# Issuing two weight scalings of a two-layer trunk behind the fourth token tile's rows

## The chip, the cores and the metric

The kernel runs on one core of a Trainium2 chip. The metric is the device time of one execution in microseconds (us); the value given is the median of the runs. A core has a matrix engine (TensorE, "PE" in the profile, its weight loads "PEld"), a vector engine (VectorE, "DVE"), an activation engine (ScalarE, "ACT"), a general engine (GpSimd, "POOL") and an engine that issues the loads and stores here (SyncE, "SP"). Each engine works through its own list of instructions; between engines they wait on semaphores.

## The reference

The input x has 512 tokens of 1024 features. Two layers follow, each a token mixer and a SwiGLU feed-forward net; in front of each sits an RMS normalization and behind each another, with a residual sum. Layer 0 mixes with RWKV-7, layer 1 with a spatial gating unit. The change lies in the first steps of layer 0:

```python
h = _rmsnorm(x, norm_gains[0, 0])
xx = _token_shift(h) - h
xs = h[None] + xx[None] * mix[:, None, None, :]      # six mixtures
r, k, v = jnp.einsum('cbtd,cde->cbte', xs[:3], w_rkv)
xw, xa, xg = xs[3], xs[4], xs[5]
w_raw = w0 + jnp.tanh(xw @ w1) @ w2                  # low rank, 64 wide
a = sigmoid(a0 + (xa @ a1) @ a2)                     # low rank, 64 wide
g = sigmoid(xg @ g1) @ g2
...                                                  # scan over the tokens, group norm, output gate
```

## The kernel before

The 512 tokens are handled as four tiles of 128 (TT = 4), the 1024 features as eight blocks of 128 (KT = 8). Nearly all matrix products are made of three: each factor is split into a rounded part (`whi`, `xgs`, cast on ScalarE, L183) and a rest (`wlo`, subtracted on VectorE, L184).

The function `rwkv` opens layer 0. L742 and L743 load the two low-rank weights w1 and a1 side by side into one tile `w1` (the profile calls it w). The loop at L748 goes over the four token tiles: sums of squares on ScalarE (L253), the inverse root in five small steps on both engines (`rc`, `rh`, `rr`, `rm`, `rt`, `ry`, L260 to L274), and then the scaled rows `hn`. Their left half is made by VectorE in two pieces of 256 columns (L753), the right half by ScalarE (L754). TensorE transposes the rows in eight blocks (`ptr`, L283); VectorE copies the first four out to `h` with the gains (L762), ScalarE the other four (L760). `h` holds all tokens with the features on the partitions, so what reads a block of `h` over all tokens needs all four tiles.

Behind the loop the feature vectors are turned (`vecT`), and `omix` = 1 − mix is formed (L775). At L802 to L805 the low-rank weights are scaled by the mixing factors, once by `omix` and once by `mix`, into two tiles `w1m` of 128 x 1024 on VectorE: the token shift is taken into the weights, so that h times the first plus shifted h times the second is the mixture times the weight. TensorE adds up the 32 products in `lora` (L809), the first 16 with the first tile, the last 16 with the second; ScalarE's tanh and a split give `hid`, which `early` multiplies with the second low-rank weights (`wa`, loaded at L900 and L901 through one buffer, split as `wa2h` and `wa2l`).

`g_hidden` (L837) then loads and splits the gate weight (`wraw` from `rwkv_g`, and its last 32 columns `g1b`, split as `g1s`) and makes its mixture block by block: `xs` on ScalarE and VectorE (L782, L783), split as `xgs`, multiplied into `gA` and `gB`. After it come the mixtures for k and r (`xsp`), with the weights of `rwkv_w_rkv` (`wraw`), and `proj`.

The order of each engine's instructions isn't the order of the text. A planner lays out the whole program once, while it is built, from its own estimates of when operands and loads will be there; on the chip each engine then keeps to its list, whether or not a load has landed. Two calls bind it. `tc.keep_in_program_order(x)` puts x behind the instruction that the text has last before it on the same engine. `with tc.issue_after(y)` puts what the block issues on y's engine behind y. Both bind the order of issue only and add no wait for the end of an instruction. Before the change each of the two scalings is bound by the first call: the first behind `omix`, the second behind the first.

Of the kernel before, what the change touches and what calls it, by code (L numbers as in the profile page):

```python
# [10 lines left out]
AF = mybir.ActivationFunctionType  # L11
ALU = mybir.AluOpType

P = 128
T = 512
D = 1024
KT = D // P
# [116 lines left out]
class Trunk:  # L134
# [551 lines left out]
    def rwkv(self, x0):  # L686
        nc, i, tc = self.nc, self.i, self.tc
        v, a, g = nc.vector, nc.scalar, nc.gpsimd
        mm = nc.tensor.matmul
        with ExitStack() as ctx:  # L690
# [14 lines left out]
            def e2(name, shape=(P, 2, T), dt=F32):  # L705
                return rp.tile(list(shape), dt, name=name, tag="e2", bufs=E2)

            def s4(name, shape, dt=F32):
                return self.slot(shape, dt, name)
# [31 lines left out]
            w1 = s4("w1", [P, KT, 2, 64])  # L741
# [6 lines left out]
            for tt in range(TT):  # L748
                hn = e2("hn", (P, D))
                s = [self.sumsq(x0[tt][:, c:c + 512], hn[:, c:c + 512]) for c in (0, 512)]  # L750
                y = self.rsqrt1(s[1], self.part(s[0], 1.0 / D, RMS_EPS), 1.0 / D)
                for c in (0, 256):
                    v.tensor_scalar(hn[:, c:c + 256], x0[tt][:, c:c + 256], y[:, 0:1], None, op0=ALU.mult)  # L753
                a.activation(hn[:, 512:1024], x0[tt][:, 512:1024], AF.Copy, scale=y[:, 0:1])  # L754
                for q, srcs in enumerate(self.rows_T(hn, lambda n: self.bank("pe", n))):
                    for kt, src in srcs:
                        dst = h[kt // 2][:, kt % 2, 1 + tt * P:1 + (tt + 1) * P]
                        gn = self.vec["g00"][:, kt:kt + 1]
                        if q:
                            a.activation(dst, src, AF.Copy, scale=gn)  # L760
                        else:
                            v.tensor_scalar(dst, src, gn, None, op0=ALU.mult)  # L762
# [39 lines left out]
            w1m = [s4("w1m", [P, KT, 2, 64]) for _ in range(2)]  # L802
            for t, m in ((w1m[0], omix), (w1m[1], self.vec["mix"])):
                mv = m[:, 3 * KT:5 * KT].rearrange("p (j k) -> p k j", j=2).unsqueeze(3)
                tc.keep_in_program_order(v.tensor_tensor(t, w1, mv.broadcast_to([P, KT, 2, 64]), op=ALU.mult))  # L805
            acc = self.bank("pt", "lora")
            for j, src in enumerate((hk, hs)):
                for kt in range(KT):
# [650 lines left out]
```

## Time and profile before

| | us |
|---|---|
| median of 3 runs (lowest to highest) | 1314.23 (1310.39 to 1314.66) |
| the profiled execution, its time | 1314.73 |
| its span, first to last instruction | 1313.0 |
| TensorE busy (share of the span) | 1254.3 (96%) |
| TensorE weight loads | 1092.0 (83%) |
| VectorE | 989.0 (75%) |
| ScalarE | 739.2 (56%) |
| GpSimd | 159.6 (12%) |

A row of the timeline gives the start (us from the span's start), the time that it took (of several merged instructions: first start to last end), the engine, the line of the kernel, the operation, output and inputs by name with their shapes, the count, and in brackets the idle time of the engine just before it with what ended it. SPq is SP's queue, whose rows are loads being issued. A row of the table by stretches gives for a stretch of time its length and each engine's busy time (with the count of instructions), the clock granted to TensorE as a share of full speed, the mean busy share of the 16 DMA engines and the GB/s that they moved. Consecutive instructions of an engine overlap somewhat in their records, so that the step from one start to the next is shorter than a duration.

### The profile page before, as it was taken

The page shows a single profiled execution, that of the slowest core. Times are in us where ns is not written, and L with a number is a line of the kernel's source. Part 1 is how long each engine was busy: PE and PEld are TensorE (multiplying, and loading weights), DVE is VectorE, ACT ScalarE, POOL GpSimd, SP SyncE. Part 2 cuts the span into 40 slices and gives each one's busy share as a digit, 9 for nine tenths or more (in the row PEclk, how much of TensorE's full clock was granted, in tenths as well). Part 3 has the DMA queues.
Part 4 walks back from the last instruction along what each step waited for, and adds up shares of the span by engine and source line. Part 5 has one row for each costly group of instructions (what it writes and reads, how often), then busy time and mean ns, then how long its engine had stood idle before and what let it go on. Part 6 is the DMA issues. An engine that isn't in the chain of part 4 may idle for free.

```text
span 1313.0 us, 24498 instructions
## 1 busy us (share of the span) xinstructions
PE 1254.3 (96%) x9692; PEld 1092.0 (83%) x9692; DVE 989.0 (75%) x1613; ACT 739.2 (56%) x1303; POOL 159.6 (12%) x300
## 2 busy tenths in 40 slices
PE   5999999989888999999999999999999999999998
PEld 3667799978776798989998878878898999998876
DVE  6975766477955679868779986575689777788985
ACT  7986785586544355435455555643464454456553
POOL 0000284566100004100000000020002000000000
PEclk9999999899979999999999999999999999999999
DMA  5136595222133325243344423243440433444322
GB/s 163 33 102 170 148 222 156 82 75 62 61 113 120 114 65 161 59 134 98 97 145 145 128 65 112 88 137 97 145 114 0 129 99 108 117 124 150 113 65 81
DMA packets 219379, 144.29 MB, mean 110 GB/s; under 512 B 67920, under 2 KB 193408, under 8 KB 219264
## 3 DMA queue, kind: packets, MB, share of 16 engines
q1 hardware_dynamic: 217968, 138.01, 36.5%
q0 software_dynamic: 1296, 4.72, 1.1%
q8 instruction: 76, 1.25, 0.4%
q14 instruction: 39, 0.32, 0.1%
HBM read 128.54 MB, written 14.16 MB: 109 GB/s over the span
## 4 chain that ended last, share of the span: by engine, by line
PE 63%; DVE 10%; DMA 2%; ACT 2%; issue 2%; SPq 1%; POOL 0%; DVEq 0%; ACTq 0%
PE acc L208 24%; PE Q L208 9%; PE gu L208 6%; PE Z L208 6%; PE R L208 6%; PE u L208 3%; DVE wlo L184 2%; PE gh L1136 1%; DVE wsum L411 1%; PE mp L1129 1%; PE Yp L1178 1%; DMA wq<-in_ffn_w_up_dram 1%; PE ptr L283 1%; DVE x L339 1%; PE lm L1021 1%
## 5 line engine op out<-in xcount | busy, mean ns | idle before, releaser
L184 DVE TENSOR_TENSOR wlo<-wraw,whi 128x1024 fp32r<-128x1024 f32 x83 | 103.1, 1246 | 69.1 <-ACT whi L183 68.7
L208 PE MATMUL Q<-bc,whi 128*128 128x256 f32 x816 | 147.5, 281 | 2.9 <-ACT hn L455 2.9
L183 ACT CAST whi<-wraw 128x1024 fp32r<-128x1024 f32 x83 | 86.9, 1049 | 101.7 <-PE acc L208 17.0
L208 PE MATMUL acc<-whi,ablk 128*128 128x512 f32 x448 | 141.5, 395 | 2.7 <-DVE acc L640 2.7
L208 PEld LDWEIGHTS Q<-bc,whi 128*128 128x128 f32 x816 | 125.6, 189 | 3.7 <-ACT hn L455 3.5
L183 ACT CAST whi<-wsum 128x1024 fp32r<-128x1024 f32 x68 | 71.0, 1051 | 89.1 <-PE Q L208 30.7
L208 PE MATMUL Q<-bc,wlo 128*128 128x256 f32 x408 | 114.4, 281 | 0.0
L208 PE MATMUL gu<-hT,whi 128*128 128x256 f32 (+1 forms) x480 | 109.3, 322 | 0.2 <-DVE hT L65 0.2
L208 PEld LDWEIGHTS acc<-whi,ablk 128*128 128x128 f32 x448 | 84.2, 188 | 23.1 <-ACT hn L638 1.8
L208 PE MATMUL Z<-bc,whi 128*128 128x256 f32 x544 | 101.0, 284 | 2.0 <-DVE bc L184 2.0
L208 PE MATMUL R<-bc,whi 128*128 128x256 f32 x544 | 99.2, 281 | 0.0
L184 DVE TENSOR_TENSOR wlo<-wsum,whi 128x1024 fp32r<-128x1024 f32 x68 | 82.3, 1222 | 18.5 <-ACT whi L183 17.3
L183 ACT CAST whi<-wq 128x1024 fp32r<-128x1024 f32 x51 | 53.5, 1050 | 70.9 <-PE R L208 22.9
L208 PE MATMUL acc<-wlo,ablk 128*128 128x512 f32 x224 | 88.6, 395 | 1.5 <-DVE wlo L184 1.4
L208 PEld LDWEIGHTS Z<-bc,whi 128*128 128x128 f32 x544 | 85.0, 191 | 2.2 <-DVE bc L184 2.2
L208 PEld LDWEIGHTS gu<-hT,whi 128*128 128x128 f32 x480 | 79.3, 188 | 8.7 <-issue 0.7
L208 PE MATMUL proj<-xsp,whi 128*128 128x512 f32 x256 | 83.5, 406 | 2.9 <-ACT r L830 2.9
L184 DVE TENSOR_TENSOR wlo<-wq,whi 128x1024 fp32r<-128x1024 f32 x51 | 64.9, 1274 | 27.3 <-ACT whi L183 27.2
L208 PEld LDWEIGHTS R<-bc,whi 128*128 128x128 f32 x544 | 84.3, 189 | 0.4
L208 PE MATMUL Z<-bc,wlo 128*128 128x256 f32 x272 | 77.2, 284 | 2.2 <-DVE wlo L184 2.2
L208 PEld LDWEIGHTS Q<-bc,wlo 128*128 128x128 f32 x408 | 77.1, 189 | 0.0
L208 PE MATMUL R<-bc,wlo 128*128 128x256 f32 x272 | 76.6, 282 | 0.0
(377 smaller groups left out, 3207.3 us busy)
## 6 DMA issues: line engine op xcount, KB each, us to landing
wc<-in_ffn_w_down_dram SPq DMA_DIRECT2D x38, 512.0 KB, 3.9
wq<-in_ffn_w_gate_dram SPq DMA_DIRECT2D x68, 256.0 KB
wq<-in_ffn_w_up_dram SPq DMA_DIRECT2D x68, 256.0 KB, 4.7
wraw<-in_rwkv_w_rkv_dram SPq DMA_DIRECT2D x24, 512.0 KB, 5.4
wraw<-in_sgu_w_in_dram SPq DMA_DIRECT2D x16, 512.0 KB, 4.0
wraw<-in_ffn_w_gate_dram SPq DMA_DIRECT2D x10, 512.0 KB
wraw<-in_ffn_w_up_dram SPq DMA_DIRECT2D x10, 512.0 KB, 3.8
x<-in_x_dram SPq DMA_DIRECT2D x8, 512.0 KB, 3.6
```

Source lines behind the costliest of these rows:

```text
L183: self.nc.scalar.copy(hi, src)
L184: self.nc.vector.tensor_tensor(lo, src, hi.bitcast(F32), op=ALU.subtract)
L208: self.nc.tensor.matmul(out, l, r, start=start, stop=stop, skip_group_check=resumed)
L283: self.nc.tensor.transpose(pt[:, j * P:(j + 1) * P], xt[:, kt * P:(kt + 1) * P], self.ident)
L339: v.scalar_tensor_tensor(xts[tt][:, c], f, y[:, 0:1], xts[tt][:, c], op0=ALU.mult, op1=ALU.add)
L411: v.tensor_tensor(s, x, y, op=ALU.add)
L1021: mm(lm[:, cc * P:(cc + 1) * P], st[:, cc].rearrange("p n t -> p (n t)"), mv[:, cc, :, hd, :], start=True, stop=True)
L1129: mm(mp[:, cc * P:(cc + 1) * P], bdT[:, q * NC + 4 * hh + cc].rearrange("p h t -> p (h t)"), mt[:, cc, :], start=True, stop=True)
L1136: mm(gh[:, cc * P:(cc + 1) * P], mt[rows, cc, :], bx[rows, 0:2, cc, :], start=True, stop=True)
L1178: mm(yp[yr, yc], MV[hh, q][:, cc, 1, hd, :], su[:, q, hd, :], start=True, stop=True)
```

## The change

The loop keeps the last scaled-row instructions in a list, `scaled`: its first entry is VectorE's second piece, its second entry ScalarE's half. After the loop it holds those of the fourth tile. Each of the two scalings is traced in a block that puts it behind the first entry, in place of being pinned in the order of the text.

```diff
@@ -750,8 +750,8 @@
                 for c in (0, 256):
-                    v.tensor_scalar(hn[:, c:c + 256], x0[tt][:, c:c + 256], y[:, 0:1], None, op0=ALU.mult)
-                a.activation(hn[:, 512:1024], x0[tt][:, 512:1024], AF.Copy, scale=y[:, 0:1])
+                    scaled = [v.tensor_scalar(hn[:, c:c + 256], x0[tt][:, c:c + 256], y[:, 0:1], None, op0=ALU.mult)]
+                scaled.append(a.activation(hn[:, 512:1024], x0[tt][:, 512:1024], AF.Copy, scale=y[:, 0:1]))
@@ -802,7 +802,8 @@
             for t, m in ((w1m[0], omix), (w1m[1], self.vec["mix"])):
                 mv = m[:, 3 * KT:5 * KT].rearrange("p (j k) -> p k j", j=2).unsqueeze(3)
-                tc.keep_in_program_order(v.tensor_tensor(t, w1, mv.broadcast_to([P, KT, 2, 64]), op=ALU.mult))
+                with tc.issue_after(scaled[0].ins):
+                    v.tensor_tensor(t, w1, mv.broadcast_to([P, KT, 2, 64]), op=ALU.mult)
```

## The prediction

> **What bounds the kernel now.** I read the page's head first, then the table by stretches, then the first 40 us instruction by instruction, one engine at a time.
>
> ```profile
> span 1313.0 us, 24498 instructions
> PE 1254.3 (96%) x9692; PEld 1092.0 (83%) x9692; DVE 989.0 (75%) x1613; ACT 739.2 (56%) x1303; POOL 159.6 (12%) x300
> ```
>
> TensorE is busy 1254.3 us of 1313.0, so 58.7 us of its idle time is all that a change of order could remove. The table by stretches (PE, PEld, DVE, ACT, POOL busy, granted clock, DMA share, GB/s) says where it lies:
>
> ```profile
> 0.00:80.00 80.00, 61.55 (x228) 40.27 (x229) 62.77 (x129) 69.62 (x132) 2.93 (x27) 1.00 0.30 89
> 80.00:430.00 350.00, 328.38 (x4042) 278.72 (x4040) 231.52 (x428) 217.02 (x434) 112.69 (x242) 0.96 0.45 122
> 430.00:1313.00 883.00, 864.35 (x5423) 773.03 (x5423) 694.66 (x1058) 452.54 (x738) 43.99 (x31) 1.00 0.36 107
> ```
>
> In the first 80 us PE idles 18.5 us, and ScalarE is busy 69.62 of 80. The changed instructions all run in the first 24 us. VectorE there:
>
> ```profile
> 13.41 0.20 DVE L273 SCALAR_TENSOR_TENSOR rt<-rr,rm 128x1 f32<-128x1 f32 x1
> 13.80 1.23 DVE L805 TENSOR_TENSOR w1m<-w,omix 128x1024 f32<-128x1024 f32 x1 [0.18 <-DMA w<-in_rwkv_a_dram]
> 14.94 1.22 DVE L805 TENSOR_TENSOR w1m<-w,vecT 128x1024 f32<-128x1024 f32 x1
> 16.07 0.21 DVE L273 SCALAR_TENSOR_TENSOR rt<-rr,rm 128x1 f32<-128x1 f32 x1
> 16.20 0.15 DVE L274 SCALAR_TENSOR_TENSOR ry<-rt,rr 128x1 f32<-128x1 f32 x1
> 17.39 1.23 DVE L184 TENSOR_TENSOR wlo<-wraw,whi 128x1024 fp32r<-128x1024 f32 x1 [1.03 <-ACT whi L183]
> 18.53 0.42 DVE L184 TENSOR_TENSOR g1s<-g1b,g1s 128x256 fp32r<-128x256 f32 x1
> 18.87 0.15 DVE L274 SCALAR_TENSOR_TENSOR ry<-rt,rr 128x1 f32<-128x1 f32 x1
> 18.94 1.14 DVE L753 TENSOR_SCALAR hn<-x,ry 128x256 f32<-128x256 f32 x4
> 19.98 1.22 DVE L184 TENSOR_TENSOR wlo<-wraw,whi 128x1024 fp32r<-128x1024 f32 x1
> 21.12 0.42 DVE L184 TENSOR_TENSOR wa2l<-wa,wa2h 128x256 fp32r<-128x256 f32 x1
> ```
>
> The two scalings (w1m) hold VectorE from 13.80 to 16.07, in front of the last steps (rt, ry) of the inverse roots of the third and fourth token tile. The scaled rows (hn, four pieces, two per tile) come only at 18.94, also behind a weight split (wlo) that waits for ScalarE. ScalarE in the same time:
>
> ```profile
> 12.51 1.14 ACT L760 ACTIVATE h<-ptr,vecT 128x128 f32<-128x128 f32 x4
> 16.31 1.04 ACT L183 CAST whi<-wraw 128x1024 fp32r<-128x1024 f32 x1 [2.66 <-DMA wraw<-in_rwkv_g_dram]
> 17.26 0.40 ACT L183 CAST g1s<-g1b 128x256 fp32r<-128x256 f32 x1
> 17.57 0.72 ACT L754 ACTIVATE hn<-x,ry 128x512 f32<-128x512 f32 x1
> 18.88 1.05 ACT L183 CAST whi<-wraw 128x1024 fp32r<-128x1024 f32 x1 [0.59 <-DMA wraw<-in_rwkv_w_rkv_dram]
> 19.83 0.40 ACT L183 CAST wa2h<-wa 128x256 fp32r<-128x256 f32 x1
> 20.14 0.72 ACT L754 ACTIVATE hn<-x,ry 128x512 f32<-128x512 f32 x1
> 20.76 1.12 ACT L760 ACTIVATE h<-ptr,vecT 128x128 f32<-128x128 f32 x4
> 22.20 1.14 ACT L760 ACTIVATE h<-ptr,vecT 128x128 f32<-128x128 f32 x4 [0.32 <-PE ptr L283]
> 23.21 1.35 ACT L782 ACTIVATE xs<-h,omix 128x512 f32<-128x512 f32 x2
> 26.23 0.41 ACT L183 CAST wa2h<-wa 128x256 fp32r<-128x256 f32 x1 [1.66 <-DMA wa<-in_rwkv_a_dram]
> 26.54 1.13 ACT L183 CAST xgs<-xs 128x512 fp32r<-128x512 f32 x2
> ```
>
> Two waits for loads stand out, each put in front of rows work in an in-order queue: 2.66 us for the gate weight, 1.66 us for the second piece of wa. And PE and SP:
>
> ```profile
> 18.34 3.82 PE L283 MATMUL ptr<-ident,hn 128*128 128x128 f32 x16 [5.87 <-ACT hn L754]
> 23.67 14.01 PE L809 MATMUL lora<-h,w1m 128*128 128x512 f32 x32 [1.51 <-DVE h L762]
> ```
>
> ```profile
> 21.79 0.47 SPq L900 DMA_DIRECT2D wa<-in_rwkv_w_dram  x1
> 22.31 0.59 SPq L901 DMA_DIRECT2D wa<-in_rwkv_a_dram  x1
> ```
>
> PE waits 5.87 us for the rows of the last two tiles, transposes them in 3.82 us, waits 1.51 us for the copies h and then has the 32 low-rank matmuls (lora) to run for 14 us. What limits after that:
>
> ```profile
> 24.00:38.00 14.00, 14.00 (x35) 6.26 (x34) 11.82 (x18) 10.95 (x18) 0.00 (x0) 1.00 0.09 28
> 38.00:76.00 38.00, 38.00 (x156) 26.55 (x156) 34.59 (x49) 36.40 (x60) 0.00 (x0) 1.00 0.15 46
> 76.00:80.00 4.00, 1.08 (x7) 0.64 (x6) 0.81 (x1) 3.97 (x5) 0.00 (x0) 1.00 0.00 0
> 80.00:84.00 4.00, 4.00 (x11) 2.85 (x10) 1.61 (x3) 3.99 (x5) 0.00 (x0) 0.57 0.44 131
> ```
>
> PE and ScalarE are both full from 38 to 76, and at 76 to 80 PE stands still while ScalarE works 3.97 of 4: it is ScalarE that is behind. So a start that is earlier for PE alone is given back at 76; only ScalarE's chain, which starts in earnest at 26.54, carries a gain to the end. From 80 on PE is the fuller engine, and a shift is passed on.
>
> **The change part by part.** No instruction is added or removed, no load moved by hand. Two ordering edges go (each scaling pinned behind the instruction written before it) and two come (each behind the second VectorE piece of the fourth tile's rows). They order the issue only, and both ends are on VectorE, so no new wait between engines arises. The list `scaled` also keeps the ScalarE piece, unused. The planner then lays out the whole program anew, which no row of before can show; the terms are worked out with before's durations.
>
> *VectorE gets 16.07 − 13.80 = 2.27 us back.* The third tile's ry then comes 0.13 us (16.07 to 16.20) after the rt that starts at about 13.6, near 13.75, in place of 16.20. With the second ry (0.07 to the next start) and four pieces at 1.14 us the rows end near 15.1 in place of 20.08. Behind them the two scalings take their 2.27 us to about 17.4. They are first read by lora.
>
> *ScalarE's half of the rows*, two times 0.72, fits into the 2.66 us in which it waits for the gate weight, if the planner puts it ahead of that cast. I take it that it does: the reason that it stood behind was an ry 2.3 us late, and the free time starts at 13.65, as ry comes. After 16.31 ScalarE then has cast and g1s (to 17.57), eight copies h (1.12 + 1.14, transposes having ended near 18: about 14 plus 3.82), the second cast (0.95 to the next start, loaded by 18.88) and wa2h (0.31): 17.57 + 2.26 + 0.95 + 0.31 = 21.1, in place of 23.21, for the first xs. That is 2.1 us.
>
> *PE:* the last VectorE copies h (eight, 0.35 each alone, half overlapped) come behind the scalings, from 17.4 or 18: lora can start between 19.6 and 21.1 in place of 23.67, the later if the gate weight's wlo and g1s (18.87 − 17.39 = 1.48 us) go first. That is 2.6 to 4.1 us for PE, but PE is not what is late at 76.
>
> *What is late next:* the second wa load. Its issue at 21.79 follows wa2l (21.12 + 0.42), which frees the one buffer, and it lands at 26.23, 4.4 us behind its issue. wa2l needs wa2h, which follows a cast that waits for its own load until 18.88. So wa2h can't come much before 19.83, nor wa2l before some 20.2; the load would be issued near 20.9 and land near 25.4. If wa2h keeps its place between xs and xgs, ScalarE gains 0 to 0.8 us. If the planner puts the xgs casts first, they come 1.67 us (3.33 less the wait) after 21.1, at 22.8, and the gain is 3.7 us. Between 0 and 3.7 I take 1.0: the order of before is the nearest row there is, and it has wa2h in front.
>
> *Moved past on other queues:* SP's next weight load waits for the gate weight's buffer, which wlo releases at 18.62 (17.39 + 1.23). With the scalings ended by 17.4, wlo can run at the same time as before, so SP loses nothing. Nothing on POOL moves. w1's slot is freed some 1.3 us later, at 17.4; I cost that at nothing, as VectorE's first xgs split is at 27.19.
>
> *Sum:* −1.0 us. The profiled execution took 1314.73 us (span 1313.0 and 1.7 around it); it is 0.5 above the median of the runs, 1314.23. So 1313.7 for a like execution, and 1313.2 against the median. By what a measurement of this kernel can tell from no change (0.3%, 3.94 us), the same.
>
> One thing could bend this sum. The stop at 76 is followed by 4 us at a granted clock of 0.57, in which 4 × 0.43 = 1.7 us of work is lost. Should ScalarE's gain close part of the stop, these 1.7 us would be saved as well. The Trainium skill, "TensorE: Matmul & The Clock Gate", section "What's actually happening", has the array's clock halved after about one idle window of some 3.4 us on a free-running count. The trace agrees as far as it goes: an idle time of about that length, then about half the clock. By that rule the sum would be −1.0 or −2.7, by the plain shift −1.0.
>
> **The rivals.**
>
> *A. The wait stays where it is.* If the planner still takes the gate weight to be there at 13.65, its cast stays ahead and ScalarE's rows stay at 17.57 and 20.14. For: the cast is ready in the plan before ry in before's order. Against: ry is ready 2.3 us sooner. PE starts earlier, ScalarE doesn't; 0 us: 1314.2.
>
> *B. Scalings in front of the copies.* If all else keeps its place, the 2.27 us stand between the rows (20.08) and the copies h, and lora starts at 25.9. For: they are ready at that very moment. Against: the hole at 13.8 has to be filled by something. ScalarE would be held up by as much: 1314.2 + 2.3 = 1316.5.
>
> *C. Slower: the new layout costs a chain later on.* Near 412 the path to the end runs through a store and a load back:
>
> ```profile
> 411.88 2.66 DMA od<-ob
> 414.59 3.54 DMA oraw<-od
> ```
>
> PE idles 21.6 us from 80 to 430 in such places. If the end of the mixing layer is laid out differently and one more such pair comes to lie bare, it costs 6.2 us: 1320.4. It decides once over 3.9 of the 6.2 us are uncovered. For: the plan is made anew for 24498 instructions. Against: the operations and their dependences there are the same.
>
> *D. Faster: everything carries.* xgs first (−3.7) and the stop at 76 short enough for the full clock (−1.7): 1314.2 − 5.4 = 1308.8. For: both waits in the ScalarE rows are for order's sake only. Against: the load of wa lies in between.
>
> **How the numbers follow.** Forecast 0.50, A 0.13, B 0.06, C 0.15, D 0.16. The likeliest gives 1313.2, with 1310.5 (−3.7) to 1315.5 (no gain, and 1.3 us for small shifts in the plan) as its own range, and 0.10 of its 0.50 with the 1.7 us of clock on top, at 1311.5. For 8 in 10 the range must reach into C and D: 1307.5 to 1319.5. Faster: D and 0.03 of the forecast's end, 0.19. Slower: C and 0.01 of B, 0.16. Same: 0.65.
>
> **What would show it.** On VectorE, w1m behind the last hn, both before 18; rt, ry and hn of tiles three and four near 14 to 15. On ScalarE, hn ahead of the whi at 16.3, and xs near 21. lora from about 20 to 21. Then a wait for wa, longer than 1.66 us, before xgs, which starts no earlier than 25. A stop of PE near 76 to 80, hardly shorter. The prediction is wrong if xgs starts before 24 and the time falls with it, if whi still stands ahead of hn, or if stretches beyond 80 us differ by more than the first one.

## The result and the profile after

| | before | after |
|---|---|---|
| median of 7 runs, us (lowest to highest) | 1312.70 (1310.37 to 1314.73) | 1318.52 (1316.18 to 1323.38) |
| ratio, with its 95% interval (not the quotient of the two medians, which is 1.0044) | | 1.0053 [1.0037, 1.0069] |
| the profiled execution, us | 1314.73 | 1316.18 |

The kernel became slower by 5.8 us, where 1.0 us faster was forecast. The two profiled executions differ by 1.5 us only: that of before is the slowest of its seven, that of after the fastest of its seven. So the profiles show places and not the whole size.

The first 21 us went as forecast. Timeline of the kernel after, VectorE:

```profile
13.73 0.28 DVE L274 SCALAR_TENSOR_TENSOR ry<-rt,rr 128x1 f32<-128x1 f32 x2
13.93 1.14 DVE L753 TENSOR_SCALAR hn<-x,ry 128x256 f32<-128x256 f32 x4
14.98 1.22 DVE L806 TENSOR_TENSOR w1m<-w,omix 128x1024 f32<-128x1024 f32 x1
16.12 1.22 DVE L806 TENSOR_TENSOR w1m<-w,vecT 128x1024 f32<-128x1024 f32 x1
17.25 1.12 DVE L762 TENSOR_SCALAR h<-ptr,vecT 128x128 f32<-128x128 f32 x4
```

The scaled rows hn start at 13.93 in place of 18.94, and the scalings w1m stand behind them. ScalarE:

```profile
13.91 1.33 ACT L754 ACTIVATE hn<-x,ry 128x512 f32<-128x512 f32 x2 [0.20 <-DVE ry L274]
15.69 1.05 ACT L183 CAST whi<-wraw 128x1024 fp32r<-128x1024 f32 x1 [0.44 <-DMA wraw<-in_rwkv_g_dram]
...
20.87 1.34 ACT L782 ACTIVATE xs<-h,omix 128x512 f32<-128x512 f32 x2
23.04 1.28 ACT L183 CAST xgs<-xs 128x512 fp32r<-128x512 f32 x2 [0.83 <-DVE xs L783]
...
26.36 0.41 ACT L183 CAST wa2h<-wa 128x256 fp32r<-128x256 f32 x1 [1.21 <-DMA wa<-in_rwkv_a_dram]
```

The rows fill the wait for the gate weight, xs comes 2.3 us earlier, and the first two casts xgs now stand ahead of wa2h. TensorE:

```profile
14.34 3.67 PE L283 MATMUL ptr<-ident,hn 128*128 128x128 f32 x16 [1.80 <-DVE hn L753]
20.93 15.40 PE L810 MATMUL lora<-h,w1m 128*128 128x512 f32 x32 [2.92 <-DVE h L762]
35.77 1.03 PE L208 MATMUL gA<-xgs,whi 128*128 128x512 f32 x2
```

The first gA of before stands at 37.11:

```profile
37.11 1.02 PE L208 MATMUL gA<-xgs,whi 128*128 128x512 f32 x2
```

So TensorE is 1.3 us ahead at the first gA. It has worked through lora without a stop until then: lora starts 2.7 us sooner, but its 32 matmuls take 15.40 us in place of 14.01. ScalarE, whose gain was forecast at 1.0, is 2.1 us ahead at its first cast xsp, 36.32 in place of 38.41. What takes more than this away lies behind it. The table by stretches of the kernel after (TensorE, weight loads, VectorE, ScalarE, GpSimd, granted clock, DMA share, GB/s):

```profile
72.00:90.00 18.00, 13.60 (x47) 9.44 (x46) 13.19 (x16) 14.24 (x18) 0.00 (x0) 0.81 0.33 88
90.00:165.00 75.00, 75.00 (x391) 56.34 (x390) 44.90 (x53) 48.16 (x65) 6.23 (x13) 1.00 0.59 147
165.00:430.00 265.00, 242.65 (x3631) 213.91 (x3631) 176.00 (x364) 160.24 (x361) 108.15 (x230) 0.97 0.42 114
430.00:475.00 45.00, 42.96 (x238) 37.23 (x237) 31.45 (x84) 24.09 (x63) 0.60 (x1) 0.96 0.39 119
```

The same stretches of before, where they differ most:

```profile
72.00:90.00 18.00, 15.08 (x58) 11.01 (x57) 11.49 (x15) 17.37 (x23) 0.00 (x0) 0.91 0.26 75
...
430.00:475.00 45.00, 44.82 (x267) 39.29 (x267) 31.25 (x82) 22.76 (x58) 0.00 (x0) 1.00 0.42 125
```

Two places stand out. From 72 to 90 TensorE gets through 47 matmuls in place of 58, at a granted clock of 0.81 in place of 0.91; from 430 to 475 it is busy for 1.9 us less. At the first place the planner has laid out other work. Timeline of the kernel after, ScalarE, then VectorE, then TensorE:

```profile
74.91 1.15 ACT L959 ACTIVATE tw<-tw,tiny 128x1024 f32<-128x1024 f32 x1
76.08 1.28 ACT L929 ACT_TABLE_LOAD   x1
77.38 0.69 ACT L929 ACTIVATE tws<-w,halfb 128x512 f32<-128x512 f32 x1
77.96 1.03 ACT L183 CAST whi<-wraw 128x1024 fp32r<-128x1024 f32 x1
78.89 0.59 ACT L831 COPY r<-proj 128x512 f32<-128x512 f32 x1
```

```profile
78.09 0.69 DVE L934 TENSOR_SCALAR tws<-tws 128x1024 f32<-128x1024 f32 x1 [3.71 <-ACT tws L929]
78.82 2.34 DVE L937 TENSOR_TENSOR_SCAN cum<-rmask,tws 128x512 f32<-128x512 bf16 x2
81.08 1.20 DVE L184 TENSOR_TENSOR wlo<-wraw,whi 128x1024 fp32r<-128x1024 f32 x1
```

```profile
79.53 1.22 PE L208 MATMUL proj<-xsp,whi 128*128 128x512 f32 x2 [2.83 <-ACT r L831]
82.33 0.80 PE L208 MATMUL proj<-xsp,wlo 128*128 128x512 f32 x1 [1.58 <-DVE wlo L184]
```

The decay of the second block of features (its tanh tws at L929, its add and its two scans at L934 and L937) is now ahead of what TensorE waits for: the tanh, with a reload of ScalarE's tables, in front of the cast whi and the copy r, and the scans in front of the rest wlo. The reload is not an extra one: before has one at 79.66, behind its copy r. Before, the same tws came at 85.76 and the scans at 87.49 on VectorE, and wlo followed its cast directly:

```profile
79.19 1.23 DVE L184 TENSOR_TENSOR wlo<-wraw,whi 128x1024 fp32r<-128x1024 f32 x1 [3.22 <-ACT whi L183]
...
85.76 0.69 DVE L933 TENSOR_SCALAR tws<-tws 128x1024 f32<-128x1024 f32 x1
...
87.49 2.33 DVE L936 TENSOR_TENSOR_SCAN cum<-rmask,tws 128x512 f32<-128x512 bf16 x2
```

So TensorE has two stops where it had one. The last proj is issued at 164.47 in place of 162.44: 1.3 us ahead has become 2.0 behind. At the second place TensorE stops twice, where before it did not stop (after, TensorE):

```profile
461.45 0.85 PE L208 MATMUL gu<-hT,whi 128*128 128x256 f32 x4 [1.35 <-ACT hT L63]
462.99 0.39 PE L208 MATMUL gu<-hT,whi 128*128 128x256 f32 x1 [0.69 <-DVE hT L65]
```

### The profile page after: what moved, and what is told of

Same layout as the page of the kernel before. It is cut to its first block, busy times and chain, and to the rows that moved or that the text cites. A ratio compares the mean times of both kernels' runs of the same rounds, so it can differ in the third digit from the quotient of the medians.

```text
span 1314.5 us, 24492 instructions
## 1 busy us (share of the span) xinstructions
PE 1254.9 (95%) x9692; PEld 1092.3 (83%) x9692; DVE 989.5 (75%) x1613; ACT 739.5 (56%) x1303; POOL 151.2 (12%) x300
## 4 chain that ended last, share of the span: by engine, by line
PE 64%; DVE 9%; issue 2%; ACT 2%; DMA 2%; POOL 0%; SPq 0%; DVEq 0%; ACTq 0%
PE acc L208 24%; PE Q L208 9%; PE Z L208 7%; PE gu L208 7%; PE R L208 6%; PE u L208 3%; DVE wlo L184 2%; PE gh L1137 1%; DVE wsum L411 1%; PE Yp L1179 1%; DMA wq<-in_ffn_w_up_dram 1%; PE lm L1022 1%; DVE x L339 1%; PE ptr L283 1%; PE mp L1130 1%
## 5 line engine op out<-in xcount | busy, mean ns | idle before, releaser
L208 PE MATMUL gu<-hT,wlo 128*128 128x256 f32 (+1 forms) x240 | 76.8, 323 | 0.0
```

What stands on the lines that cost most here:

```text
L208: self.nc.tensor.matmul(out, l, r, start=start, stop=stop, skip_group_check=resumed)
```

## The experiments

Theory: the opening is not to blame; the order that the planner laid out behind it is, above all the early decay work near 77 us, and perhaps the stops near 461. Rivals: the new opening itself costs; the loss is spread over many small moves.

A change in the source would make the planner lay out everything anew. So each kernel here has the issue order of all five engines given, instruction by instruction, by edges that order the issue alone and add no wait:

```diff
         build(tc, ins, outs[0])
+        _recorded(nc, tc)    # per engine: each instruction of a list behind the one before it
...
+            if prev is not None:
+                tc.add_manual_dep(ins[name], prev, mybir.DependencyInfo(mybir.DependencyClass.NoSync, ...))
```

The lists are put together from the orders of before and after, with cuts where both have issued the same instructions: about 40 us (behind lora), about 100 us and about 430 us (end of the mixing layer). Below, "old" is the order of before and "new" that of after. Each of the groups e1 to e4, e5 to e8 and e9 to e11, and e12 by itself, is set against runs of before on the same chip. The ratios are of 5 to 12 executions of each kernel.

| | to 40 | 40 to 100 | 100 to 430 | from 430 | ratio [95%] | matmuls 72 to 90 | last proj at |
|---|---|---|---|---|---|---|---|
| before | old | old | old | old | 1 | 58 | 162.44 |
| e1 | new | old | old | old | 1.0001 [0.9987, 1.0016] | 71 | 159.67 |
| e12 | new | old, 4 moved | old | old | 1.0034 [1.0017, 1.0051] | 42 | 166.53 |
| e8 | new | new | old | old | 1.0033 [1.0018, 1.0049] | 46 | 164.87 |
| e3 | new | new | new | old | 1.0036 [1.0016, 1.0056] | 44 | 165.53 |
| e7 | new | new | new | new | 1.0052 [1.0030, 1.0075] | 41 | 167.35 |
| e5 | new | new, 1 moved | new | new | 1.0042 [1.0025, 1.0058] | 51 | 163.91 |
| e9 | new | new, 2 moved | new | new | 1.0016 [1.0001, 1.0031] | 65 | 160.75 |
| e10 | new | new, 2 moved | new | old | 1.0010 [0.9994, 1.0026] | 61 | 162.05 |
| e4 | new | old | old | new | 1.0006 [0.9991, 1.0021] | 69 | 159.96 |
| e2 | old | new | new | new | 1.0099 [1.0078, 1.0119] | 42 | 167.92 |
| e6 | new | old | new | new | 1.0065 [1.0040, 1.0090] | 61 | 166.44 |

The last two columns are from one profiled execution each, and they vary: the kernel after and e7 have the same order, and show 47 and 41 matmuls and the last proj at 164.47 and 167.35.

**e1, the new opening alone.**

```diff
-order: new to the end
+order: new to 40 us, old from there
```

> The opening (to about 40 us) in the order of the changed kernel, all engines behind it in the recorded order of the kernel before. Theory (the opening gains 1.3 us, and what loses is the new order of the work behind it): about 1311.4 us against 1312.7 before, ratio 0.999. Rival (the earlier opening is itself what costs, by meeting later waits or the clock gate at another time): as the changed kernel, about 1318.5, ratio 1.0045.

1311.12 us, before at 1310.88. The theory holds: with the old order behind it the new opening costs nothing. It gains nothing that can be measured either. The stretch by the table, the stop there and the last proj:

```profile
72.00:90.00 18.00, 16.66 (x71) 12.26 (x70) 11.60 (x14) 16.21 (x21) 0.00 (x0) 1.00 0.31 88
```

```profile
78.32 0.73 PE L208 MATMUL proj<-xsp,whi 128*128 128x512 f32 x2 [1.29 <-ACT r L831]
...
159.67 0.40 PE L208 MATMUL proj<-xsp,wlo 128*128 128x512 f32 x1
```

The stop has shrunk from 2.92 to 1.29, the clock stays at 1.00, and TensorE is 2.8 us ahead of before's profile at the last proj. TensorE had no lead in the opening here: lora took 17.08 us, and the first gA stands at 37.39, behind before's 37.11. ScalarE was 1.7 us ahead, with its first xsp at 36.72. A lead of 2.8 us is not in the time of the twelve executions.

**e2, the old opening and the new order behind it.**

```diff
-order: old to the end
+order: old to 40 us, new from there
```

> The mirror image: the opening as before, all engines behind it in the recorded order of the changed kernel. Theory: slower than the changed kernel by the 1.3 us of the opening, about 1319.8 us, ratio 1.0054. Rival (the opening costs): as before, 1312.7, ratio 1.000.

1323.98 us. The new order is slow with the old opening too, so the loss doesn't hang on the opening; but it is 4 us more than the theory gave (6 by the ratio), and why is open. Two orders put together can make a fault of their own, as in e6 below.

**e3 and e4, the new order in the middle alone and at the end alone.**

```diff
 e3
-order: new to the end
+order: new to 430 us, old from there
 e4
-order: new to the end
+order: new to 40 us, old to 430 us, new from there
```

> Opening and middle (40 to 430 us) in the order of the changed kernel, the rest, where layer 0's output projection ends and its feed-forward net begins, as before. Theory (two places cost: the stop of TensorE near 80 us, 3.3 us, and the gaps at 460 us, 3.7 us): 1318.5 - 3.7 = 1314.8 us, ratio 1.0016. Rival A (only the stop near 80 counts): 1318.5. Rival B (only the gaps at 460): about 1311.4.

> Opening in the order of the changed kernel, the middle (40 to 430 us) as before, the rest from 430 us in the order of the changed kernel. Theory (two places cost): 1318.5 - 3.3 = 1315.2 us, ratio 1.0019. Rival A (only the stop near 80 counts): about 1311.4. Rival B (only the gaps at 460): 1318.5.

1316.27 and 1311.51 us. The middle carries 0.0036 of the 0.0053. The order from 430 on, alone, gives 1.0006, which can't be told from e1's 1.0001. e4 came out 3.7 us under what the theory expected and at its rival A: by itself, the place at 461 isn't seen in the time.

**e7, the changed order held, nothing moved.**

```diff
+order: new to the end, as recorded
```

> The changed kernel with its whole order held as recorded, nothing moved: what the holding itself does. Theory: nothing, so the ratio of the changed kernel, 1.0037 to 1.0069, and the two stops of 2.8 and 1.6 us again. Rival (the holding costs time): above 1.007; then the runs with held orders can't be set against the changed kernel itself.

1320.45 us, 1.0052 beside the changed kernel's 1.0053: holding the order costs nothing that can be seen.

**e8 and e6, the stretch from 40 to 100 alone, and all but it.**

```diff
 e8
+order: new to 100 us, old from there
 e6
+order: new to 40 us, old to 100 us, new from there
```

> The changed kernel's opening and its order to about 100 us, then the order of before to the end: the suspected stretch alone. Theory (the stretch at 70 to 85 us carries the loss): two stops near 80, 44 to 47 matmuls from 72 to 90, and 3 to 5 us over before, near 1316 (1.0025 to 1.004). Rival (spread over 100 to 430, or the gap at 460): within 1 us of before, 1312.

> The changed kernel's order as recorded, with the order of before from 40 to about 100 us alone on VectorE, ScalarE and PE; everything from there on as in the changed kernel. Theory (the re-planned order at 70 to 85 us carries the loss): one stop of 1.3 to 2.0 us near 78, 66 to 71 matmuls from 72 to 90, and the time near 1312 with before at 1312 (ratio 1.000). Rival (the loss is spread over 100 to 430): most of it stays, 1316 to 1318.

e8: 1315.34 us, as the theory says; that one stretch costs (1.0033 − 1.0001) × 1312, or 4.2 us, give or take 2.8 by the two intervals. e6: 1320.77 us, where 1312 was expected, a miss. A row of ScalarE and one of TensorE show why it tells nothing on the stretch:

```profile
107.03 0.69 ACT L958 ACTIVATE tws<-ssp,tiny 128x512 f32<-128x512 f32 x1 [13.93 <-PE ssp L956]
```

```profile
108.38 1.12 PE L956 MATMUL ssp<-tws,bones 128*128 128x512 f32 x2 [1.45 <-ACT tws L954]
```

The new order behind 100 us does not fit the old order ahead of it: ScalarE stands for 13.93 us on a norm (ssp) that TensorE issues late, and new stops follow. The mixture made a fault of its own.

**e5, one instruction moved in the changed order.**

```diff
 VectorE, near 78 us
+wlo <- wraw, whi
 tws <- tws + 1.0
 cum <- scan(tws)   (x2)
-wlo <- wraw, whi
```

> The changed kernel with its own order held as recorded on every engine, and one instruction moved: near 78 us VectorE does the weight's rest (wlo) ahead of the decay's add and its two scans, not behind them. Theory (the wlo behind 3.0 us of decay work is what costs): PE's second stop at 82, 1.58 us in the changed kernel, is gone, the stretch 72 to 90 us has 4 to 6 more matmuls than its 47, and the time falls by 2 to 3 us below the e7 run, near 1316. Rival A (ScalarE's order in front of it costs, or the rest of the middle): the second stop goes but the time stays within 1 us of e7, near 1318.5. Rival B (the decay's scans are needed early): another stop opens behind them, 1318.5 or more.

1315.96 us, ratio 1.0042 [1.0025, 1.0058] beside e7's 1.0052. The second stop is gone, four matmuls more than after's 47 stand in the stretch, and the clock is still at 0.81 there, behind the first stop alone, which is 2.83 us long as in the kernel after:

```profile
72.00:90.00 18.00, 15.17 (x51) 10.93 (x50) 11.97 (x14) 15.11 (x20) 0.00 (x0) 0.81 0.25 70
```

The intervals of e5 and e7 overlap; this half alone can't be told from nothing.

**e9 and e10, both halves moved.** e9 is e5 with, on ScalarE:

```diff
 ScalarE, near 77 us
 tw  <- Ln(tw)
-tws <- tanh(w)
 whi <- wraw
 r   <- proj
+tws <- tanh(w)
```

e10 is e9 with the old order from 430 us on.

> As e5 (changed order as recorded, the weight's rest ahead of the decay's add and scans), and on ScalarE the decay's tanh (tws) is issued behind the next cast and the copy of r, not ahead of them: both halves of what was planned early near 77 us are put behind what PE waits for. Theory (this early decay work is what the re-planned middle costs): one stop near 77 to 79, 1 to 1.7 us long, at a clock of 0.9 or more, over 60 matmuls from 72 to 90, and the time about 3 to 4 us under the changed kernel, ratio 1.000 to 1.003 (1312 to 1315 with before at 1311). Rival A (the stop's length is without effect, as PE's idle time is filled elsewhere): ratio 1.004 to 1.005 as e5 and e7. Rival B (decay work now late): a new stop of over 1 us between 90 and 110, as in e6, and 1.005 or more.

> As e9, with the order of before from about 430 us on. Theory (two places, near 80 and near 460, carry the whole loss): 1 to 2 us under e9, level with before or up to 2 us faster (ratio 0.9985 to 1.001), with over 44.5 us of PE work from 430 to 475. Rival (the place near 460 costs nothing in the time): as e9.

1314.07 us (1.0016) and 1311.58 us (1.0010 [0.9994, 1.0026]), before at 1311.25. Two instructions put back regain 0.0036 of e7's 0.0052. e9, table and stops:

```profile
72.00:90.00 18.00, 16.08 (x65) 11.39 (x64) 12.71 (x15) 15.55 (x20) 0.00 (x0) 1.00 0.29 82
```

```profile
77.87 0.73 PE L208 MATMUL proj<-xsp,whi 128*128 128x512 f32 x2 [0.83 <-ACT r L831]
85.50 0.50 PE L208 MATMUL proj<-xsp,wlo 128*128 128x512 f32 x1 [1.05 <-DVE wlo L184]
```

Here the cast that feeds the second wlo is late in its turn, but neither stop is followed by a lower clock. e10 differs from e9 by less than the intervals tell apart, in the direction of the theory, though at 0.8 us by the ratios it is below the 1 to 2 us that it expected (the medians are 2.5 us apart).

**e11, the kernel before once more.**

```diff
+                # scaled by the mixing factors
```

> The kernel before, with a comment added: a second profile of it. Theory (the clock's fall at 80 in the first profile is not in every execution): the stop at 76 is as long, 2.9 us, and 58 to 66 matmuls stand from 72 to 90, with the clock in that stretch between 0.9 and 1.0. Rival: stop and clock as in the first profile, 58 and 0.91.

One execution: 1308.33 us, 6.4 under the first profiled execution, with the same stop and the same low clock behind it. The rival holds:

```profile
72.00:90.00 18.00, 15.18 (x57) 10.88 (x57) 11.50 (x15) 17.44 (x23) 0.00 (x0) 0.91 0.26 75
```

So both profiles of before have the one stop, and what sets these two executions apart lies later: they issue the last proj at 162.44 and 162.66, and the load back that rival C shows (oraw) at 414.59 and 409.32. By the second place this execution is 5.3 of its 6.4 us ahead.

**e12, the suspected cause by itself.** The order of e1 with four instructions moved, one on ScalarE and three on VectorE; TensorE's order is untouched:

```diff
 ScalarE, near 77 us
 tw  <- Ln(tw)
+tws <- tanh(w)       (with a table load)
 whi <- wraw
 r   <- proj
...
-tws <- tanh(w)
 VectorE
+tws <- tws + 1.0
+cum <- scan(tws)   (x2)
 wlo <- wraw, whi
...
-tws <- tws + 1.0
-cum <- scan(tws)   (x2)
```

> The order of e1 (the changed kernel's opening, then the order of before: ratio 1.0001), with the suspected cause put in by itself: on ScalarE one tanh of the decay (tws) ahead of the cast and the copy of r near 77 us, on VectorE its add and two scans ahead of that weight's wlo. TensorE's order is untouched. Theory (this early decay work is what costs): ScalarE's copy of r comes 1.3 to 2 us later, PE's stop near 78 grows from 1.3 to about 3 us, a second one of 1 to 2 us on wlo follows, and of the 71 matmuls from 72 to 90 no more than 52 are left; the time rises by 3 to 5 us over e1, ratio 1.0025 to 1.004. Rival A (the loss needs the many other moves of the new order): ratio under 1.001. Rival B (half of it: the stop costs, but the decay's work is then out of the way later): 1.001 to 1.0025.

1317.37 us, before at 1312.93: 1.0034 [1.0017, 1.0051], against e1's 1.0001 [0.9987, 1.0016]. Table, TensorE's stops with its last proj, and ScalarE:

```profile
72.00:90.00 18.00, 12.35 (x42) 8.27 (x41) 11.94 (x15) 14.74 (x19) 0.00 (x0) 0.81 0.24 69
```

```profile
81.20 1.07 PE L208 MATMUL proj<-xsp,whi 128*128 128x512 f32 x2 [3.93 <-ACT r L831]
84.00 0.79 PE L208 MATMUL proj<-xsp,wlo 128*128 128x512 f32 x1 [1.73 <-DVE wlo L184]
...
166.53 0.40 PE L208 MATMUL proj<-xsp,wlo 128*128 128x512 f32 x1
```

```profile
76.58 1.15 ACT L959 ACTIVATE tw<-tw,tiny 128x1024 f32<-128x1024 f32 x1
77.74 1.28 ACT L929 ACT_TABLE_LOAD   x1
79.04 0.69 ACT L929 ACTIVATE tws<-w,halfb 128x512 f32<-128x512 f32 x1
79.62 1.04 ACT L183 CAST whi<-wraw 128x1024 fp32r<-128x1024 f32 x1
80.56 0.59 ACT L831 COPY r<-proj 128x512 f32<-128x512 f32 x1
```

The table load and the tanh hold cast and copy back by 79.62 − 77.74 = 1.9 us, and the scans hold wlo back until 82.75. Some of the first stop's growth is chance: ahead of the moved instructions ScalarE was already 0.9 us later than in e1's profile (L959 at 76.58 in place of 75.70), and TensorE 0.25 us. TensorE's stops grow from 1.29 to 3.93 + 1.73 us, so by 4.4; the last proj is 6.9 us later than in e1. Some 2.2 us of the difference is left to the low clock behind the stops, besides the 0.25 us. In the time it is (1.0034 − 1.0001) × 1312 = 4.3 us, give or take 2.9. Within the intervals, four instructions out of 24498 make as much of a loss as the whole stretch in e8. The cause is shown by taking it out (e9, 1.0016 against e7's 1.0052) and by putting it in (e12 against e1).

No version here beats the kernel before: e1, e4 and e10 are level with it.

## Why the prediction was wrong, step by step

The time rose where a small fall was forecast. The median, 1318.52, still lies in the wide range, 1307.5 to 1319.5, but only because rival C had stretched it, and C's place was another: that is luck.

- *VectorE, ScalarE's half of the rows, PE:* right up to the start of lora. The rows ended near 15 (15.07), xs came at 20.87 (21.1 forecast), lora at 20.93 (19.6 to 21.1). That lora could take longer was in no term: 15.40 to 17.08 us in the other twelve profiles, 14.01 in both of before. In seven of the twelve the granted clock is under 1 while its first matmuls run, as in e5, 0.63 from 20 to 24 us.
- *What is late next, the second wa load:* ScalarE's gain was 2.1 us at the first xsp, in the range of 0 to 3.7, where 1.0 was taken. The working was partly wrong: wa2l came at 21.93, later than before's 21.12, and the load landed no sooner (wa2h at 26.36). ScalarE gained because two xgs casts were laid ahead of wa2h, at 23.04, which the forecast had as its better case; the wait for wa, 1.21 us, came behind them. The 1.3 us at the first gA have another cause: TensorE had no stop between lora and gA, so they are the 2.7 us of lora's sooner start less the 1.4 us that it took longer.
- *The sum took the opening's gain as carried to the end:* this step was wrong by its 1.0 us and more. e1 has ScalarE's gain, and with it the shorter stop and the full clock of rival D, a lead of 2.8 us at 162 us by the profiles, and its time is 1.0001 × before, from 1.7 us faster to 2.1 us slower. "From 80 on PE is the fuller engine, and a shift is passed on" fits the delay of e12 (4.1 us behind before's profile at the last proj, 4.4 us in the time), and not this lead. Each sets one profile beside a ratio of several executions, so that no rule follows.
- *The planner lays out the whole program anew:* this is the term that failed most. The forecast named it, gave it zero, and 1.3 us for small shifts. What it put at nothing measured 4.2 us for the stretch from 40 to 100 us (e8), and 4.3 us for the four instructions in it (e12).
- *Rival C* had the right kind of cause at 0.15, and the wrong place: a store and load back near 412, 6.2 us. The place was the stop at 76 to 80 that the forecast had shown. It was used there for what could be saved by closing it, and not for what an order with ScalarE and VectorE a little less well laid would add to it, though ScalarE was busy 3.97 of 4 us there, with TensorE's next matmul waiting on its last instruction.
- *The clock sentence:* a low clock behind the stop did count, with the other sign. From 72 to 90 us the granted clock was 0.81 in place of 0.91, so that (1 − 0.81) × 18 = 3.4 us of clock were lost in place of 1.6. The second stop isn't needed for that: e5 has the first alone, and 0.81 as well.
- The rest of the loss, from 1.0033 (e8) to 1.0053, is not settled. The stops at 461 are 2.04 us of idle time, which would be 0.0016; e3 against e7 fits that (1.0036 and 1.0052), e4 against e1 shows 0.0005 of it, and the intervals hold both.
- Where the lead of e1 goes is open as well, and one profile each can't tell. At the load back (oraw) e1, at 409.81, is 4.8 us ahead of the first profile of before and 0.5 us behind the second (e11), although these two were 0.2 us apart at the last proj. Executions of one kernel part by more than the lead there.

## What to carry to other kernels

When a list planner lays out a whole program, an edit at its start is two edits: the one written and a new order of everything behind it. Look in the profile of before for stops that end on an engine which is itself full, as at 76 to 80 here; a little more work in front of what ends them can go into the time, with the low clock behind it (four instructions, 4.3 us here), so that such a place deserves a rival of its own, with a price. Afterwards, give the old order back piece by piece: that tells which half of the edit cost the time. Then put the suspected cause in by itself, since a mixture of orders can make a fault of its own (e6).

## What the runs showed of the hardware

**The low clock behind a stop of TensorE does not go by the length of the stop alone.** Stops of 2.63 to 2.92 us near 79 us were followed by it every time. Shorter ones went both ways: 0.83 and 1.05 (e9), 1.29 (e1) and 1.98 us (e4) had a clock of 1.00 right through, 1.06 us (e10) did not. e10's stop, and the stretch behind it:

```profile
78.87 0.73 PE L208 MATMUL proj<-xsp,whi 128*128 128x512 f32 x2 [1.06 <-ACT r L831]
```

```profile
80.00:84.00 4.00, 4.00 (x12) 3.14 (x11) 3.12 (x5) 3.99 (x6) 0.00 (x0) 0.57 0.44 131
```

The same stretch of e1, at the full clock with 19 matmuls in place of 12:

```profile
80.00:84.00 4.00, 4.00 (x19) 3.29 (x18) 2.35 (x4) 4.00 (x6) 0.00 (x0) 1.00 0.44 132
```

The Trainium skill, "TensorE: Matmul & The Clock Gate", section "What's actually happening", has a window of activity that runs freely; that one stop of 1.06 us brings the low clock and one of 1.98 us does not agrees with that. That section also asks for an idle window of about 3.4 us. Here no stop near 79 us but e12's 3.93 was that long, and the measurement decides: 1.06 us can be enough.

Where it came, the loss had two sizes. From 72 to 90 us the clock was 0.91 in before, e6, e10 and e11, and 0.81 in after, e2, e3, e5, e7, e8 and e12, which is 1.6 or 3.4 us of clock lost; it was 1.00 in e1, e4 and e9. Stops of about the same length had either: 2.92 us 0.91 (before), 2.83 us alone 0.81 (e5).

**A low clock came at the start of lora too, and the profile doesn't always show it.** In e5 the granted clock was 0.63 from 20 to 24 us, and lora took 15.70 us in place of before's 14.01. In the kernel after, the table has 1.00 there, yet the first four matmuls of lora took 3.38 us, where four at before's mean pace (14.01 / 32) take 1.75. That it was the low clock there as well is likely, and not shown.

**A reload of ScalarE's tables** took 1.30 us from its start to the start of what it was for (77.74 to 79.04 in e12), right behind the end of the instruction ahead of it (76.58 + 1.15 = 77.73). The Trainium skill, "ScalarE: Activation LUTs", section "What ACT_TABLE_LOAD costs", gives about 1.28 us for the load, as here, and about 2.66 us with a drain; no drain is seen here.
